# A diagonal matrix product in a chunked scan: the decayed state goes into PSUM, and the results are evacuated as copies

## The chip, the cores and the metric

The kernel runs on one core of one Trainium2 chip. The metric is device time of one execution in microseconds (us), as a median over runs. The engines are TensorE (PE in the profile, with its weight loads as PEld), VectorE (DVE), ScalarE (ACT), GpSimd (POOL) and SyncE (SP), which issues the DMAs.

## The reference, cut to what matters

The program is a two-layer encoder over 512 tokens and 1024 channels. The change sits in layer 0, in the RWKV-7 time mixing: 8 heads of 64 channels, two directions, with a recurrence over the tokens for a 64 x 64 state per head and direction.

```python
def step(S, inp):
    r_t, w_t, k_t, v_t, kk_t, a_t = inp
    sa = jnp.einsum('dbhvk,dbhk->dbhv', S, kk_t)
    S = (S * w_t[..., None, :] - sa[..., :, None] * (kk_t * a_t)[..., None, :]
         + v_t[..., :, None] * k_t[..., None, :])
    return S, jnp.einsum('dbhvk,dbhk->dbhv', S, r_t)
...
_, ys = lax.scan(step, S0, seqs)
ys = jnp.moveaxis(ys, 0, 2)
y = ys[0] + jnp.flip(ys[1], axis=1)
```

Beside it, in the same layer, stand an input projection, a Hyena branch (long convolutions through transforms) and an output projection; then come a gated MLP, an embedding, a second layer with attention, and a second MLP and embedding.

## The kernel before, in words

Channels lie on the 128 partitions, tokens along the free axis. `mixer0` is the whole mixing part of layer 0; everything after it is a chain of large products in float32r (three matmuls for one product of split numbers, tile names `g`, `whi`, `wlo`). In `mixer0` the code doesn't write its instructions in a fixed order. A class `Pace` keeps estimates of when each engine will be free and each tile be ready, and `drive` writes, step by step, either a piece of the **main line** (dense products: the input projection, the transforms, per-layer embeddings, the early part of the output projection `out_early`, the inverse transforms `inverse`) or a stage of one of the **chains** of small steps. `in_order` then holds every engine to the order in which it was written. So a change of one chain's instructions moves the places of all others in the four queues. SBUF work tiles there come from a pool of slabs (`SLABS`, name `w`), PSUM tiles from a pool of 8 banks (name `b`).

The recurrence is computed in chunks of 64 tokens. For two heads at a time (`m` = 0 to 3) and both directions, `rwkv_prep` makes the decayed vectors, `inverse_ab` inverts triangular matrices, and `scan(m)` goes through 8 chunks, each of which needs the state of the one before. `next_scan` lets at most two scans be open. When a scan is over, `rwkv_out(m)` makes its part of the output projection's input.

One chunk of `scan`, before, in the order in which it is written (`uv` holds state and values, `x` what was prepared, `ch` a PSUM tile with three slots for each direction, `yp` the outputs' PSUM tile; "product" is a group of four 64-row or 128-row matmuls, one for each direction and head):

1. first product (`m1` with `uv`) into slot 0; DVE copies it to `r0` (L1281);
2. output product of the old state into `yp`; DVE makes `sp`, the state times its decay (L356, two instructions, one per head; the decay is in `pcs`);
3. second product (`zt` with `r0`) into slot 1; ACT writes one head's negated result into `uv`, DVE the other's (L1296);
4. third product (`x` with `uv`) into slot 2; DVE adds `sp` to it and writes the new state into the next chunk's `uv` (L356, two instructions);
5. the rest of the outputs into `yp`.

A helper records most operations, so that in the profile all `self.mm` have line 350, all `self.tt` line 356 and all `self.act` line 359; tile names tell them apart. The tile `r0` is called `r` in the profile, as buffer numbers are left out.

Of the kernel before, what the change touches and what calls it, by code (L numbers as in the profile page):

```python
# [10 lines left out]
F32 = mybir.dt.float32  # L11
# [21 lines left out]
# ---------------------------------------------------------------- layout of the weights  # L33
# [14 lines left out]
# row tiles of layer 0's output projection: those of its early part, and the others  # L48
# [20 lines left out]
def _kc(n):  # L69
    """Row tiles of weights in a chunk of n column tiles."""  # L70
    return (8, 4, 2, 2)[n - 1]
# [13 lines left out]
# columns of the packed per-channel parameters: name -> number of columns  # L85
# [32 lines left out]
# ---------------------------------------------------------------- constants of the shapes  # L118
# [23 lines left out]
def _constants():  # L142
# [18 lines left out]
    # transforms at the frequencies (2f+1)pi/1024, f < 256; even and odd times apart, which gives those of 511 - f  # L161
# [4 lines left out]
    fwd = parts.reshape(4, 4, P, 2, P)  # part, tile of times, time, fc, f  # L166
    c["dft_f"] = np.ascontiguousarray(fwd.transpose(3, 2, 0, 1, 4)).reshape(2, P, 2048)
    inv = parts.transpose(0, 2, 1).reshape(4, 2, P, S)  # part, fc, f, time
    c["dft_i"] = np.ascontiguousarray(inv.transpose(1, 2, 0, 3)).reshape(2, P, 2048)
    # filter features and decay window  # L170
# [10 lines left out]
def _rpb_table(rpb):  # L181
    """Relative position bias as each (16-column query block, head) reads it, both by columns of the grid;
    -1e30 outside the window."""
# [16 lines left out]
    t = np.stack(out, axis=2).reshape(8, 2, P, 3, 256)  # pair, head, q, table, key  # L200
# [3 lines left out]
# ---------------------------------------------------------------- the kernel  # L204
class Pace:
    """Estimates of when what is written so far will have run. The order in which the rest is written follows them;
    nothing that is computed depends on them."""
# [15 lines left out]
    @staticmethod  # L223
    def area(x):
        """Name, first and last row, first and last column."""
        size = math.prod(x.tensor.shape[1:])
        p, f = divmod(x.offset, size)
        p1, f1 = p, f
        for i, (step, n) in enumerate(x.ap):
            if i == 0 and step == size:  # L230
                p1 += n - 1
            elif step < 0:
                f += step * (n - 1)
            else:
                f1 += step * (n - 1)
        return x.tensor.name, (p, p1, f, f1)
# [5 lines left out]
    def ready(self, tiles):  # L242
        """When all that is written into the tiles so far is there."""
# [4 lines left out]
    def after(self, marks, area, e, own):  # L248
        """The end of the accesses in marks to an area, seen by engine e; those of its own count only if own."""
# [10 lines left out]
    # TensorE runs at half its clock after a stretch of this many us in which it streamed less than so many columns  # L260
# [5 lines left out]
    def density(self, t):  # L266
        """Columns streamed in the last TICK us before t."""
# [48 lines left out]
class Kern:  # L316
# [5 lines left out]
    # -- helpers  # L322
# [26 lines left out]
    def mm(self, out, lhsT, rhs, start=True, stop=True):  # L349
        return self.nc.tensor.matmul(out, lhsT, rhs, start=start, stop=stop)  # L350
# [10 lines left out]
    def split(self, h, l, src, scale=None):  # L361
        """h + l = src (* scale), each in float32r."""
# [12 lines left out]
    def load_split(self, src, width, dt=F32):  # L375
        """One chunk of weights: from DRAM and into its two parts."""
# [7 lines left out]
    def gemm(self, wname, g, k0, k1, xs, evac, then=None):  # L384
        """then: what goes in between after two chunks of weights."""
# [23 lines left out]
    def rsqrt_rows(self, pool, srcs, col, scale, eps):  # L409
        """For each of srcs [128 channels, tokens]: 1 / sqrt(scale * (sums over the channels of col) + eps),  # L410
        back on all of those channels, in PSUM."""
# [23 lines left out]
    def norm(self, h, gain):  # L435
        """Splits gain * h into float32r parts; returns them, the tile of 1 / rms per token, on all partitions,
        and what computes that."""
# [25 lines left out]
    def conv3(self, out, u, w, b):  # L463
        """Centred depthwise convolution of width 3 over the tokens."""
# [9 lines left out]
    # -- the whole  # L474
# [42 lines left out]
    def mixer0(self):  # L517
# [5 lines left out]
        # tiles in DRAM  # L523
# [31 lines left out]
    SLABS = 59  # L555
    PREPS = 4

    def in_order(self, start):
        """Keeps the compute engines to the order in which everything from instruction start on is written."""
# [11 lines left out]
    # -- small helpers: slabs of SBUF, a bank of PSUM  # L571
# [9 lines left out]
    def parts(self, src):  # L581
        """A slab's two parts; the second one by GpSimd."""
# [5 lines left out]
    def stream(self, items):  # L588
        """Slabs from DRAM in their two parts, loaded and split ahead of their use. An item with two sources has its
        parts in them."""  # L590
# [37 lines left out]
    def weights(self, name, g):  # L628
        """The slabs of a group of columns."""
# [15 lines left out]
    # -- the order of the work: a main line of dense products, and chains of small steps beside it  # L645
    def start(self, prio, gen, *wait):
        """A chain of stages. It yields what its next stage waits for; of the chains whose stages can go, the one of
        the lowest prio does."""
# [3 lines left out]
    def put(self, out, in_):  # L652
        """A store, written once its data should be there, so that its queue doesn't wait."""
# [16 lines left out]
    def drive(self):  # L670
        """Stages of the chains as they can go, and the main line between them."""
# [31 lines left out]
    def both_mixers(self):  # L703
# [32 lines left out]
        # [chunk of frequencies][cosine, sine][f, 511 - f]  # L736
# [40 lines left out]
        # loads in the order of their use  # L777
# [24 lines left out]
        # 1 - mu; k_a / 2 and 1 - k_a / 2; w0 / 2, a0 / 2  # L802
# [24 lines left out]
    def norm0(self, xin):  # L827
        """The layer's input with its gains, in two parts; 1 / rms per token."""
# [30 lines left out]
    def columns(self, out):  # L859
        """A tile of columns of the input projection."""  # L860
# [986 lines left out]
```

## Time and profile before

| | |
|---|---|
| time, median of 3 runs | 1636.56 us (1633.0 to 1638.45) |
| the profiled execution | span 1633.0 us, which is also its time |
| PE busy | 1541.6 us (94%), 9296 matmuls |
| DVE busy | 1047.9 us (64%) |
| ACT busy | 681.0 us (42%) |
| POOL busy | 341.3 us (21%) |
| `mixer0` | from 0 to about 504 us; the four scans lie in 180 to 484 us |

Busy time of an engine is the sum of its instructions' times; matmuls overlap in their pipeline and their ends are modelled, so that a busy PE is not a PE at its peak. Idle time "before" a group of instructions is put down to the instruction that ended the wait. In a timeline, rows that follow each other closely are merged (`x8` is 8 instructions; a 64 x 64 float32 matmul is recorded as two).

### The profile page before, as it was taken

To read this page: it belongs to the slowest core of one execution; us is meant where nothing else is said; L and a number is where in the kernel's file an instruction comes from. 1 tells how busy PE (TensorE), PEld (TensorE's weight loads), DVE (VectorE), ACT (ScalarE), POOL (GpSimd) and SP (SyncE) were. 2 spreads that over 40 slices of the span, in tenths; PEclk is the share of its full clock that TensorE was granted. 3 is DMA by queue.
4 is the path that set the end of the run, shared out by engine and by line. 5 is a ranking of instruction groups with operands and counts; after the bars stand their busy time and mean duration, and the time that the engine had idled before them with its cause. 6 is when DMAs were issued, how large, how long until landed. Compare 5 with 4: busy or idle time off the path is not lost.

```text
span 1633.0 us, 24094 instructions
## 1 busy us (share of the span) xinstructions
PE 1541.6 (94%) x9296; PEld 1216.2 (74%) x9296; DVE 1047.9 (64%) x1740; ACT 681.0 (42%) x1082; POOL 341.3 (21%) x286
## 2 busy tenths in 40 slices
PE   7998798979898999999999989999999999999997
PEld 4675576766667888888888778777777888888886
DVE  7579868876876677534684664565666665276654
ACT  6464224333514544313443553565554442144432
POOL 3585525533721200000001322011030000000020
PEclk9999899899999999999999999999999999999999
DMA  6455638465764232222322433323112332322341
GB/s 202 136 141 137 188 105 237 136 215 157 232 214 167 100 103 90 96 99 90 103 91 96 137 116 103 106 83 123 66 65 78 103 104 90 98 88 93 110 142 65
DMA packets 116308, 200.13 MB, mean 123 GB/s; under 512 B 27729, under 2 KB 57297, under 8 KB 116194
## 3 DMA queue, kind: packets, MB, share of 16 engines
q1 hardware_dynamic: 116194, 198.59, 37.9%
q8 instruction: 73, 1.20, 0.3%
q14 instruction: 41, 0.34, 0.1%
HBM read 166.04 MB, written 30.93 MB: 121 GB/s over the span
## 4 chain that ended last, share of the span: by engine, by line
PE 76%; DVE 11%; issue 5%; ACT 3%; DMA 2%; POOL 2%; SPq 2%; POOLq 0%; DVEq 0%; ACTq 0%
PE g L350 60%; PE b L350 11%; DVE w L356 4%; DVE w L353 3%; PE m L350 1%; PE s L350 1%; PE m L1792 1%; ACT w L359 1%; POOL w L356 1%; DVE w L1168 1%; POOL rr L356 0%; ACT oh L364 0%; DVE ol L356 0%; DMA ch_d<-w 0%; POOL nacc L356 0%
## 5 line engine op out<-in xcount | busy, mean ns | idle before, releaser
L356 DVE TENSOR_TENSOR wlo<-wraw,whi 128x1024 fp32r<-128x1024 f32 x186 | 235.6, 1268 | 334.7 <-ACT whi L364 334.5
L364 ACT CAST whi<-wraw 128x1024 fp32r<-128x1024 f32 x186 | 194.2, 1044 | 426.8 <-PE g L350 410.2
L350 PE MATMUL g<-xh,whi 128*128 128x512 f32 x872 | 341.5, 392 | 5.4 <-ACT whi L364 5.4
L350 PE MATMUL g<-xl,whi 128*128 128x512 f32 x872 | 340.5, 390 | 0.0
L350 PE MATMUL g<-xh,wlo 128*128 128x512 f32 x872 | 340.3, 390 | 0.0
L356 POOL TENSOR_TENSOR w<-w 128x512 fp32r<-128x512 f32 (+2 forms) x142 | 184.0, 1317 | 166.7 <-ACT w L584 95.8
L350 PEld LDWEIGHTS g<-xh,whi 128*128 128x128 f32 x872 | 164.2, 188 | 41.2 <-ACT whi L364 5.6
L350 PEld LDWEIGHTS g<-xh,wlo 128*128 128x128 f32 x872 | 164.1, 188 | 34.9 <-DVE wlo L356 0.8
L350 PEld LDWEIGHTS g<-xl,whi 128*128 128x128 f32 x872 | 164.3, 188 | 33.7
L350 PE MATMUL b<-xh,w 128*128 128x512 f32 x464 | 172.4, 427 | 7.4 <-ACT xh L359 7.3
L356 POOL TENSOR_TENSOR nacc<-nsq 128x512 f32<-128x512 f32 x5 | 9.3, 1865 | 779.8 <-ACT nsq L359 779.8
L350 PE MATMUL b<-w 64*64 64x64 f32 (+6 forms) x1884 | 131.2, 271 | 17.5 <-DVE w L353 7.5
L350 PE MATMUL g<-hh,wlo 128*128 128x512 f32 x352 | 139.0, 395 | 0.0
L350 PE MATMUL g<-hl,whi 128*128 128x512 f32 x352 | 139.0, 395 | 0.0
L350 PE MATMUL g<-hh,whi 128*128 128x512 f32 x352 | 138.9, 395 | 0.0
L353 DVE SCALAR_TENSOR_TENSOR c<-u,prm,c 128x511 f32<-128x511 f32 x176 | 126.6, 748 | 6.9 <-ACT c L359 6.3
L350 PEld LDWEIGHTS b<-w 64*64 64x64 f32 (+4 forms) x1884 | 94.6, 142 | 44.1 <-POOL w L356 10.4
L350 PEld LDWEIGHTS b<-xh,w 128*128 128x128 f32 x464 | 91.6, 197 | 36.8 <-ACT xh L359 8.0
L359 ACT ACTIVATE c<-u,prm 128x512 f32<-128x512 f32 x88 | 70.0, 817 | 71.4 <-DVE u L356 71.4
L350 PE MATMUL b<-xl,w 128*128 128x512 f32 x232 | 95.7, 413 | 1.6 <-DVE xl L353 1.4
L356 DVE TENSOR_TENSOR w<-w 128x512 f32<-128x512 f32 (+16 forms) x127 | 88.8, 708 | 3.8 <-DMA w<-hw_d 1.0
L356 DVE TENSOR_TENSOR u<-g,rstd 128x512 f32<-128x512 f32 x104 | 71.5, 687 | 14.2 <-PE g L350 13.4
(178 smaller groups left out, 2344.0 us busy)
## 6 DMA issues: line engine op xcount, KB each, us to landing
wraw<-in_up SPq DMA_DIRECT2D x88, 512.0 KB, 3.5
wraw<-in_down SPq DMA_DIRECT2D x44, 512.0 KB, 3.4
w<-in_mix_w_in SPq DMA_DIRECT2D x52, 256.0 KB, 3.8
wraw<-in_na_w_qkv SPq DMA_DIRECT2D x24, 512.0 KB, 3.5
x<-ch_d SPq DMA_DIRECT2D x16, 640.0 KB, 5.9
ch_d<-w SPq DMA_DIRECT2D x64, 128.0 KB, 2.7
wraw<-in_gate SPq DMA_DIRECT2D x16, 512.0 KB, 3.5
tab<-in_rpb SPq DMA_DIRECT2D x8, 768.0 KB, 4.3
```

The costliest lines, as they stand in the source:

```text
L350: return self.nc.tensor.matmul(out, lhsT, rhs, start=start, stop=stop)
L353: return self.nc.vector.scalar_tensor_tensor(out=out, in0=in0, scalar=scalar, in1=in1, op0=op0, op1=op1)
L356: return (eng or self.nc.vector).tensor_tensor(out=out, in0=in0, in1=in1, op=op)
L359: return self.nc.scalar.activation(out=out, in_=in_, func=func, **kw)
L364: self.nc.scalar.copy(h, src)
L1168: nc.vector.tensor_reduce(out=x[:, i, 0:i], in_=tv, axis=AX.X, op=ALU.add)
L1792: nc.tensor.transpose(pst[:, i], sc[:, i // 2, (i % 2) * P:(i % 2 + 1) * P], ident)
```

## The change

Three things change, all in `scan` but for the size of the pool. The decayed state is no longer made by DVE: `decay(c)` lets ACT write, one chunk ahead, a matrix `dg` with the chunk's decay on its diagonal (the identity, scaled by a column of `pcs`), and a new product of `dg` with the state goes into slot 2 of `ch`, where the third product is then accumulated onto it. The copy to `r0` goes from DVE to ACT. The new state is evacuated by one copy on ACT (first head) and one on DVE (second head), in place of two additions on DVE. Only the first matmul into a bank half has its start flag now, since all slots share a bank. The pool of slabs has one fewer, since the four `dg` tiles (1 KB a partition each) are larger than the four `sp` tiles (512 bytes).

```diff
-    SLABS = 59
+    SLABS = 58
...
+        def decay(c):
+            if c < 7:
+                dg = dgs[c] = rb.tile([P, 2, P], F32, name="dg", bufs=4)
+                for d in range(2):
+                    self.act(dg[:, d], self.cst("ident"), AF.Copy, scale=self.pcs[:, m, d, c:c + 1])
+        decay(0)
...
-                    self.mm(ch[rows, d, 0], m1[d][par][:, c], uv[:, d, par, w])
+                    self.mm(ch[rows, d, 0], m1[d][par][:, c], uv[:, d, par, w], start=d == 0, group=False)
+            if c < 7:
+                dg = dgs.pop(c)
+                for d in range(2):
+                    for par, rows in both:
+                        self.mm(ch[rows, d, 2], dg[rows, d, rows], uv[rows, d, par, w], False, group=False)
...
-            nc.vector.tensor_copy(out=r0, in_=ch[:, :, 0])
+            nc.scalar.copy(r0, ch[:, :, 0])
...
-            if c < 7:
-                sp = rb.tile([P, 2, 64], F32, name="sp", bufs=4)
-                for par, rows in both:
-                    self.tt(sp[rows], uv[rows, :, par, w],
-                            self.pcs[rows, m, :, c].unsqueeze(2).to_broadcast([64, 2, 64]), ALU.mult)
...
-                    self.mm(ch[rows, d, 1], zt[d][rows, c], r0[rows, d])
+                    self.mm(ch[rows, d, 1], zt[d][rows, c], r0[rows, d], False, group=False)
...
+            decay(c + 1)
             yield uv,
...
-                        self.mm(ch[rows, d, 2], x[:, d, par, o], uv[:, d, par, w])
-                for par, rows in both:
-                    self.tt(nx[rows, :, par, wn], ch[rows, :, 2], sp[rows], ALU.add)
+                        self.mm(ch[rows, d, 2], x[:, d, par, o], uv[:, d, par, w], False, group=False)
+                nc.scalar.copy(nx[0:64, :, 0, wn], ch[0:64, :, 2])
+                nc.vector.tensor_copy(out=nx[64:128, :, 1, wn], in_=ch[64:128, :, 2])
```

In the changed file these lines stand some 10 lines lower: the copy to `r0` is L1298, DVE's negation L1308, the new state's copies L1317 (ACT) and L1318 (DVE).

How the queues move is shown at the sixth chunk of the last scan (m = 3). The PSUM tile `ch` of that chunk is `b_5419` before and `b_5529` now; brackets name the engine whose signal an instruction waits for.

PE before, from the chunk's first product (`uv,w`) to the next chunk's. `x,uv` is an output product, `r,w` the second product, `uv,x` the third; `xh` and `xl` are a piece of `out_early` from the main line.

```order
L350 MATMUL b<-uv,w 64x64 x4
L350 MATMUL b<-x,uv 64x64 x4
L350 MATMUL b<-r_5424,w 64x64 x4
L350 MATMUL b<-xh_3898,w 128x512
L350 MATMUL b<-xl_3899,w 128x512
L350 MATMUL b<-xh_3898,w 128x512
L350 MATMUL b<-xh_4419,w 128x512
L350 MATMUL b<-xl_4420,w 128x512
L350 MATMUL b<-xh_4419,w 128x512
L350 MATMUL b<-uv,x 64x64 x4
L350 MATMUL b<-x,uv 64x64 x4
L350 MATMUL b<-uv,w 64x64 x4
```

PE now, from the sixth chunk's first product to the seventh's `dg` product:

```order
L350 MATMUL b<-uv,w 64x64 x4
L350 MATMUL b<-uv,dg 64x64 x4
L350 MATMUL b<-x,uv 64x64 x4
L350 MATMUL b<-r_5538,w 64x64 x4
L350 MATMUL b<-uv,x 64x64 x4
L350 MATMUL b<-x,uv 64x64 x4
L350 MATMUL b<-uv,w 64x64 x4
L350 MATMUL b<-uv,dg 64x64 x4
```

The new product (`uv,dg`) stands between the first product and the outputs', and at this chunk the six dense matmuls that lay between the second and the third product lie elsewhere.

ACT before, from the fifth chunk's negated result to the seventh's: casts of transform and embedding tiles, copies of outputs, and one instruction of the scan for each chunk.

```order
L584 CAST w_5382<-w_5359 128x512 [waits DVE_49]
L584 CAST w_5386<-w_5360 128x512 [waits DVE_49]
L359 ACTIVATE uv_5011<-b_5368 64x2x64 [waits DVE_49,PE_49]
L359 ACTIVATE uv_5011<-b_5419 64x2x64 [waits DVE_49,PE_49]
L359 ACTIVATE uv_5011<-b_5456 64x2x64 [waits DVE_49,PE_49]
```

ACT now, the sixth chunk alone:

```order
L1298 COPY r0_5538<-b_5529 128x128 [waits PE_49]
L359 ACTIVATE uv_5095<-b_5529 64x2x64 [waits PE_49,Activation_49]
L359 ACTIVATE dg_5551<-con_58,pcs_144 128x128 x2
L584 CAST w_5554<-w_5455 128x512 [waits DVE_49]
L584 CAST w_5558<-w_5456 128x512 [waits DVE_49]
L1317 COPY uv_5095<-b_5529 64x2x64 [waits DVE_49,PE_49]
```

ACT has five instructions of the scan for a chunk in place of one, and here two casts stand ahead of its copy of the new state.

DVE before, the sixth chunk:

```order
L1281 COPY r0_5424<-b_5419 128x128 [waits PE_49]
L356 TENSOR_TENSOR sp_5430<-uv_5011,pcs_144 64x128 [waits DVE_49] x2
L1296 TENSOR_SCALAR uv_5011<-b_5419 64x2x64 [waits DVE_49,Activation_49]
L356 TENSOR_TENSOR uv_5011<-b_5419,sp_5430 64x2x64 [waits PE_49]
L356 TENSOR_TENSOR uv_5011<-b_5419,sp_5430 64x2x64
```

DVE now, the sixth chunk and the seventh's negation:

```order
L1308 TENSOR_SCALAR uv_5095<-b_5529 64x2x64 [waits DVE_49,Activation_49]
L356 TENSOR_TENSOR w_5562<-w_4914,w_4915 128x512 [waits DMAHW0_49]
L356 TENSOR_TENSOR w_5563<-w_4914,w_4915 128x512 [waits DMAHW2_49]
L1318 COPY uv_5095<-b_5529 64x2x64 [waits Activation_49]
L1308 TENSOR_SCALAR uv_5095<-b_5584 64x2x64 [waits DVE_49,Activation_49]
```

Of DVE's six instructions for a chunk two are left, and both wait for ACT: the negation as before, and the copy of the new state, whose signal comes from ACT's copy of the other head. An addition and a subtraction of the spectrum now stand between the two.

More of the change, by code (lines that the diff above doesn't have):

```diff
@@ L347, in rcst, with mm @@
         return self.rcon[:, a:b]
-    def mm(self, out, lhsT, rhs, start=True, stop=True):
-        return self.nc.tensor.matmul(out, lhsT, rhs, start=start, stop=stop)
+    def mm(self, out, lhsT, rhs, start=True, stop=True, group=True):
+        return self.nc.tensor.matmul(out, lhsT, rhs, start=start, stop=stop, skip_group_check=not group)
     def stt(self, out, in0, scalar, in1, op0, op1):
@@ L1270, in scan @@
         yts = None
+        dgs = {}
+        def decay(c):
[4 more added lines that the diff above has]
+        decay(0)
         for c in range(8):
```

## The prediction

> **What bounds the kernel now.** I read the page first: with its instructions' times added up PE is busy for 94% of the span, but the change touches only the scans, so I cut the span where scans start and end.
>
> ```profile
> span 1633.0 us, 24094 instructions
> PE 1541.6 (94%) x9296; PEld 1216.2 (74%) x9296; DVE 1047.9 (64%) x1740; ACT 681.0 (42%) x1082; POOL 341.3 (21%) x286
> ```
>
> The busy times by stretch (length, then PE, PEld, DVE, ACT, POOL, then granted clock, DMA share and GB/s):
>
> ```profile
> 0.00:180.00 180.00, 155.41 (x1101) 111.59 (x1101) 138.14 (x222) 93.00 (x161) 109.17 (x117) 0.95 0.53 155
> 180.00:252.00 72.00, 63.70 (x859) 46.68 (x858) 51.48 (x125) 19.15 (x43) 23.87 (x21) 0.95 0.54 157
> 252.00:365.00 113.00, 95.56 (x1045) 72.55 (x1043) 94.24 (x184) 39.87 (x80) 54.08 (x49) 0.91 0.62 186
> 365.00:437.00 72.00, 67.36 (x652) 51.73 (x653) 54.13 (x108) 30.40 (x63) 34.44 (x27) 0.93 0.56 174
> 437.00:504.00 67.00, 54.53 (x509) 41.24 (x507) 50.24 (x91) 21.14 (x43) 25.58 (x19) 0.96 0.62 213
> 504.00:1633.00 1129.00, 1105.09 (x5136) 892.45 (x5136) 659.69 (x1015) 477.44 (x694) 94.15 (x56) 0.99 0.30 100
> ```
>
> The last 1129 us hold no scan and keep their instructions. The four stretches with scans last 324 us: PE busy 281.2 (87%), DVE 250.1 (77%), ACT 110.6 (34%), and PE idle 42.9. PE is the fullest, DVE close behind, ACT has room. The waits of PE there (in total, times, longest) name who makes it idle:
>
> ```profile
> PE b L350 <- DVE uv L356: 11.1, 15, 3.0
> PE b L350 <- DVE w L356: 7.0, 6, 2.6
> PE b L350 <- DVE uv L1296: 6.0, 5, 2.7
> PE b L350 <- DVE r L1281: 5.5, 5, 1.9
> PE g L350 <- ACT whi L364: 5.4, 1, 5.4
> PE b L1043 <- DVE w L356: 2.8, 1, 2.8
> ```
>
> So 22.6 us (11.1 + 6.0 + 5.5) are waits for the scan's own three DVE steps, and 9.8 us (7.0 + 2.8) for other DVE work; the 5.4 us stand at the end, where the large products begin. A chain that is merely busy on DVE costs nothing where the main line fills PE; these waits are what can be won.
>
> One chunk that runs undisturbed, the sixth of the last scan, from its first product to the next one's (start, duration, engine, line, tiles, in brackets the idle time before):
>
> ```profile
> 472.75 0.77 PE L350 MATMUL b<-uv,w 128*64 128x64 f32 x8 [0.23 <-DVE uv L356]
> 473.45 0.45 PE L350 MATMUL b<-x,uv 64*64 64x64 f32 x8
> 473.55 0.29 DVE L1281 COPY r<-b 128x128 f32<-128x128 f32 x1 [0.54 <-PE b L350]
> 473.88 0.60 DVE L356 TENSOR_TENSOR sp<-uv,pcs 64x128 f32<-64x128 f32 x2
> 473.90 0.45 PE L350 MATMUL b<-r,w 64*64 64x64 f32 x8
> 474.28 0.50 PE L350 MATMUL b<-xh,w 128*128 128x512 f32 x1
> 474.39 0.27 ACT L359 ACTIVATE uv<-b 64x128 f32<-64x128 f32 x1 [3.85 <-PE b L350]
> 474.70 0.29 DVE L1296 TENSOR_SCALAR uv<-b 64x128 f32<-64x128 f32 x1 [0.22 <-ACT uv L359]
> 475.87 0.45 PE L350 MATMUL b<-uv,x 128*64 128x64 f32 x8
> 476.37 0.61 DVE L356 TENSOR_TENSOR uv<-b,sp 64x128 f32<-64x128 f32 x2 [1.38 <-PE b L350]
> 476.71 0.66 PE L350 MATMUL b<-uv,w 128*64 128x64 f32 x6 [0.15 <-DVE uv L356]
> ```
>
> Here `sp` is off the path: it ends at 474.48, before ACT's negation ends at 474.66. And a chunk with DVE's queue full, the first of the same scan:
>
> ```profile
> 440.21 2.32 DVE L356 TENSOR_TENSOR sp<-uv,pcs 64x128 f32<-64x128 f32 x2
> 442.64 0.29 DVE L1296 TENSOR_SCALAR uv<-b 64x128 f32<-64x128 f32 x1
> 442.97 6.36 DVE L356 TENSOR_TENSOR w<-w 128x512 f32<-128x512 f32 x4
> 442.99 0.45 PE L350 MATMUL b<-uv,x 128*64 128x64 f32 x8 [1.29 <-DVE uv L1296]
> 449.36 0.61 DVE L356 TENSOR_TENSOR uv<-b,sp 64x128 f32<-64x128 f32 x2
> 449.70 0.77 PE L350 MATMUL b<-uv,w 128*64 128x64 f32 x8 [3.04 <-DVE uv L356]
> ```
>
> The first wait (1.29) came from a slow `sp` ahead of the negation, and goes with `sp`; the second (3.04) from four other DVE operations ahead of the new state, and nothing in the change takes those away.
>
> **The change part by part.** The groups that it removes or that price what it adds (busy, mean ns, idle before):
>
> ```profile
> L356 DVE TENSOR_TENSOR sp<-uv,pcs 64x128 f32<-64x128 f32 x56 | 21.5, 384 | 1.3
> L356 DVE TENSOR_TENSOR uv<-b,sp 64x128 f32<-64x128 f32 x56 | 16.0, 286 | 9.3 <-PE b L350 8.2
> L1296 DVE TENSOR_SCALAR uv<-b 64x128 f32<-64x128 f32 x32 | 9.4, 294 | 12.9 <-ACT uv L359 12.2
> L1281 DVE COPY r<-b 128x128 f32<-128x128 f32 x32 | 9.2, 287 | 12.4 <-PE b L350 12.4
> L359 ACT ACTIVATE uv<-b 64x128 f32<-64x128 f32 x32 | 8.7, 270 | 120.5 <-PE b L350 104.0 <-DVE sp L356 16.5
> L1314 ACT COPY w<-b 128x256 f32<-128x256 f32 x16 | 5.2, 376 | 10.5 <-PE b L350 10.5
> L584 ACT CAST w<-w 128x512 fp32r<-128x512 f32 x53 | 31.7, 618 | 8.8 <-DVE w L356 5.0 <-DMA w<-in_mix_w_out_a 1.9 <-DMA s_d<-w 1.8
> ```
>
> 1. *The new product.* 28 groups of four (7 chunks in each of 4 scans). Four such products take PE from 473.90 to 474.28, 0.38 us: 28 x 0.38 = +10.6. They stand behind the first product, and the copy to `r0` now waits for all eight, as they share a PSUM tile; so they lie on the scan's path as well as on PE. Low end 6, if PE would else have stood waiting at some of them; high end 13, at the lower granted clock (0.91) and with some cold stretches. I take 10.6. The Trainium skill ("PSUM — Partial Sum Buffer", on bank collisions) says that two engines must not be on the same bank and quadrant at once, whatever the address, so the copy could not go ahead of the new product even with other bookkeeping; no run here shows the collision.
>
> 2. *DVE's relief.* Gone are 21.5 + 16.0 + 9.2 = 46.7 us; added are 28 copies at 0.29 (the nearest rows, 64x128 and 128x128 from PSUM, are 0.286 to 0.294) = 8.1. DVE falls from 250.1 to 211.5 us, 77% to 65% of the stretches. What PE gets of it lies between two ends: its 32.4 us of waits on DVE shrink in proportion to DVE's load (15%), -5; or the waits for `r0` (5.5) and the negation (6.0) vanish and half of those for the new state (5.5) do too, -17. The two waits of the disturbed chunk are one of each kind, so I take about the middle, -12.
>
> 3. *ACT's load.* Added are 32 copies to `r0`, 28 of the new state and 56 halves of `dg`. 128 elements in a row cost 0.27 on ACT and 256 cost 0.376; at 0.28 that makes 116 x 0.28 = +32.5 us, ACT from 34% to 44%. `dg` is written one chunk ahead and needed later than the two instructions take (0.56): its cover is the third product, which in the undisturbed chunk starts 1.2 us after ACT's negation ends. If that cover goes, the new state's copy comes late by up to 0.5 us. What is new is that the scan's copies queue behind casts of 0.62, some of which wait for a DMA. An even chance of meeting half a cast (0.44 x 0.31 us), twice a chunk, would be 7.6 us over 28 chunks; most of it falls where PE has dense work. Between 0 and 6 I take +2.
>
> 4. *The new state through two engines.* Two additions in a row took 0.61 us. Now ACT copies one half (0.27) and then DVE, which waits for ACT, the other (0.29); with the 0.04 us that the negation shows between the two (474.66 to 474.70) that is 0.60. Nothing won, nothing lost: 0.
>
> 5. *The granted clock.* The stretches ran at 0.91 to 0.96: 72 x 0.05 + 113 x 0.09 + 72 x 0.07 + 67 x 0.04 = 21.5 us of full clock lost. With a third less waiting some of it comes back: -2.5 (0 to -5).
>
> 6. *One slab fewer, and the order.* No row prices the slab. SP's queue already waits where a weight load needs a slab that PE still reads:
>
> ```profile
> SPq L599 <- PE b L350: 12.5, 10, 3.7
> ```
>
> Yet the casts of such a weight (the L584 row) waited for it only 1.9 us. 0, up to +3. The last scan's last chunk now has 35 dense units of the main line (matmuls of 512 columns) behind it on PE, before 53: 18 units at 0.23 us (474.62 to 474.85 in the same chunk) have moved ahead of it. The cover of the final `rwkv_out` gets shorter by 4.1 us; it stays covered if the inverse transform still ends later. 0, up to +4.
>
> Sum: +10.6 - 12 + 2 + 0 - 2.5 + 0 = -1.9 us on the profiled execution of 1633.0, so 1631.1. The median of the runs (1636.56) lies 3.6 above that execution; set beside it: 1634.7, and I say 1634.5.
>
> **The rivals.**
>
> *DVE was the real bound.* In the second stretch DVE is busy for 83% and PE for 85%, and every wait of PE in the list above but the last stage's 5.4 us is on DVE. The slow `sp` (its 56 took 271 to 1265 ns) speaks for a queue whose waits fall faster than its load:
>
> ```profile
> L356 DVE TENSOR_TENSOR sp<-uv,pcs x56: 271/289/1265, 188.9 to 478.2; 64x128 f32<-64x128 f32 x56
> ```
>
> Then the high ends of steps 2 and 5 hold and the 9.8 us of other waits halve: 10.6 - 17 - 4.9 - 5 + 1 = -15, 1621. Against it: the undisturbed chunk, where DVE isn't on the path but for `r0`. The Trainium skill ("SBUF — State Buffer", Who interferes with whom) has it that a DVE instruction with two SBUF inputs contends with GpSimd's reads; the trace agrees, as `sp` reads two SBUF tiles and swings by a factor of 4.7, while the copy to `r0` and the negation, which read PSUM, don't.
>
> *The two halves of the new state go side by side.* They touch different partitions. Then 0.3 us a chunk are won, 28 x 0.3 = -8.4, and the time is 1626. Against it: DVE's negation, the same pattern, waited 12.2 us for ACT's (row of L1296), and the copy's signal comes from ACT. The Trainium skill's PSUM page would let two engines work in different quadrants of a bank at once; that permits this rival, but the built order doesn't use it.
>
> *Slower: the chain gets longer than the plan thinks.* The planner compares areas, sees two halves on different partitions and reckons ACT's and DVE's copies side by side, so it expects the new state 0.3 us too early in each of 28 chunks; at chunks where it leaves no dense work between (as in the sixth of the last scan) PE stands. Price: 8.4, with +10.6 of the new product and only the proportional -5 of waits: +14, 1650. It decides from where PE's waits at the scan shrink by less than about 6 us in total. For it: ACT's negation and DVE's already run in series; against it: dense work fills most of these gaps.
>
> **How the numbers follow.** What a measurement can tell from no change here is about 0.3%, 4.9 us: 1631.7 to 1641.5 is "the same". The forecast, a balance of more PE work and fewer waits, 0.38. DVE the bound, 0.31, and side by side, 0.05, both faster: 0.36. The longer chain, 0.26, slower. Low end 1622, next to the DVE rival's 1621; high end 1648, next to the chain's 1650. The forecast's own range is 1630 to 1641.
>
> **What would show it.** In the new profile: `dg` matmuls as 224 records, each four spaced by 0.38 us (step 1); DVE in `mixer0` lower by about 38 us, PE's waits for DVE's `uv` and ACT's `r` together near 12 us in place of 22.6 (2); ACT higher by 32 us, its copies at 0.27 to 0.29 (3); DVE's copy starting after ACT's (4); a granted clock in 180 to 500 us above 0.94 (5); the first `g` matmul at 501 to 504 us. I'm wrong if other waits, on ACT's queue or on weights, take the place of those removed, or if the new order of the main line leaves a hole of several us anywhere.

## The result and the profile after

The changed kernel takes 1652.71 us (1650.82 to 1654.92), the kernel before 1635.64 us (1633.0 to 1638.45): ratio 1.0099, 95% interval 1.0080 to 1.0117. It is slower by 1%; 1634.5 was forecast. The order in which the planner wrote the new instructions makes the loss; the instructions by themselves cost next to nothing, as two runs with swapped orders show below.

The page after, to be read against the same two lines of before:

```profile
span 1651.0 us, 24581 instructions
PE 1553.8 (94%) x9520; PEld 1223.8 (74%) x9520; DVE 1008.0 (61%) x1624; ACT 711.4 (43%) x1198; POOL 337.0 (20%) x286
```

DVE fell by 39.9 us and ACT rose by 30.4, as forecast (38 and 32); PE's busy time rose by 12.2. So the edit did its work on the engines, and the span is 18 us longer all the same. Where? The stretches of the changed kernel (length, then PE, PEld, DVE, ACT, POOL, granted clock, DMA share, GB/s), the last two being all of the scans' part up to the first `g` matmul, and the rest:

```profile
180.00:252.00 72.00, 61.64 (x855) 45.16 (x846) 44.32 (x95) 25.10 (x69) 22.99 (x21) 0.95 0.52 149
252.00:365.00 113.00, 96.00 (x997) 71.02 (x997) 71.86 (x127) 44.26 (x102) 48.51 (x46) 0.86 0.53 156
365.00:437.00 72.00, 61.74 (x600) 45.63 (x600) 41.23 (x87) 31.57 (x78) 24.31 (x20) 0.88 0.64 191
180.00:522.61 342.61, 293.72 (x3236) 219.83 (x3227) 209.68 (x389) 140.29 (x341) 130.17 (x113) 0.91 0.56 173
522.61:1651.00 1128.39, 1104.56 (x5136) 891.43 (x5136) 659.42 (x1016) 477.28 (x694) 94.14 (x56) 0.99 0.30 100
```

and the same two of before:

```profile
180.00:503.99 323.99, 281.14 (x3060) 212.19 (x3059) 250.08 (x505) 110.56 (x229) 137.97 (x113) 0.93 0.59 182
503.99:1633.00 1129.01, 1105.10 (x5136) 892.46 (x5136) 659.70 (x1015) 477.44 (x694) 94.15 (x56) 0.99 0.30 100
```

The rest is the same (1128.4 against 1129.0), so all 18.6 us lie in the scans' part. PE is busy there for 12.6 us more and idle for 6.0 more (48.9 against 42.9). The new product accounts for about half of the busy time (PE is busy for 6.7 us more in e1 below, which has the product but not the new order); the granted clock fell from 0.91 to 0.86 between 252 and 365 us and from 0.93 to 0.88 between 365 and 437. PE's waits in the scans' part of the changed kernel:

```profile
PE b L350 <- DVE uv L1318: 7.5, 7, 4.1
PE b L350 <- DVE w L356: 7.1, 4, 4.3
...
PE b L350 <- DVE w L1168: 5.2, 2, 4.9
...
PE b L350 <- ACT uv L1317: 4.9, 6, 1.3
PE b L350 <- ACT dg L359: 3.3, 2, 2.0
PE b L350 <- DVE uv L1308: 2.4, 7, 0.8
```

The scan's own steps are waited for less than before: 7.5 + 4.9 + 2.4 = 14.8 us (18.1 with the 3.3 for `dg`), where `r`, negation and new state had 22.6. But waits of 4 to 5 us stand here that before did not have (its longest on DVE was 3.0): for the new state's DVE half (4.1), for other DVE work (4.3, 4.9). The 4.9 stands at the start of the first scan (182 us); the two others come in the middle, 13 us apart.

The longest wait for the new state, in the timeline of the changed kernel (start, duration, engine, line, tiles, in brackets the idle time before):

```profile
313.63 0.29 DVE L1308 TENSOR_SCALAR uv<-b 64x128 f32<-64x128 f32 x1 [2.10 <-ACT uv L359]
...
313.96 5.12 DVE L353 SCALAR_TENSOR_TENSOR w<-w,prm 128x511 f32<-128x511 f32 x4
...
314.55 0.26 ACT L1317 COPY uv<-b 64x128 f32<-64x128 f32 x1 [0.95 <-PE b L350]
...
319.06 0.33 PE L350 MATMUL b<-uv,w 128*64 128x64 f32 x2
...
321.73 1.42 DVE L356 TENSOR_TENSOR w<-b,rcon 128x256 f32<-128x256 f32 x4
...
323.17 0.29 DVE L1318 COPY uv<-b 64x128 f32<-64x128 f32 x1
...
323.52 0.69 PE L350 MATMUL b<-uv,w 128*64 128x64 f32 x6 [4.13 <-DVE uv L1318]
```

ACT's half of the new state is there at 314.81. DVE's half is one copy of 0.29 us, and it runs 8.4 us later, because 9.2 us of other work (313.96 to 323.17) stand ahead of it in DVE's queue: four operations of the Hyena branch, six of the inverse of another pair, and four multiplications by a mask (the row at 321.73). The main line's dense matmuls cover 4.4 us of that (to 319.06), and PE stands for 4.13. It stands again some 13 us later:

```profile
334.68 0.69 DVE L356 TENSOR_TENSOR w<-w,rcon 128x512 f32<-128x512 f32 x1 [3.91 <-DMA vt_d<-w]
...
337.10 2.08 PE L350 MATMUL b<-w,con 128*128 128x512 f32 x2 [4.33 <-DVE w L356]
```

for 4.33, on a chain whose DVE operation the profile puts behind a store. Now the clock around both:

```profile
314.00:319.00 5.00, 5.00 (x35) 3.84 (x34) 4.93 (x4) 0.78 (x2) 3.43 (x3) 1.00 0.19 64
324.00:328.70 4.70, 4.70 (x34) 2.88 (x32) 1.85 (x5) 1.79 (x4) 0.00 (x0) 0.50 0.75 223
328.80:332.70 3.90, 3.90 (x25) 3.22 (x25) 0.80 (x2) 3.87 (x8) 1.69 (x2) 1.00 0.27 25
337.10:342.40 5.30, 5.30 (x43) 3.52 (x45) 2.00 (x3) 1.13 (x2) 2.19 (x3) 0.50 0.67 163
342.50:346.00 3.50, 3.50 (x68) 2.71 (x64) 3.46 (x6) 1.24 (x3) 0.05 (x1) 1.00 0.78 243
310.00:346.00 36.00, 26.14 (x239) 18.89 (x239) 22.11 (x38) 11.25 (x24) 13.75 (x13) 0.81 0.47 125
```

PE is full again from 324 us on, but at half clock for 4.7 us, and again for 5.3 us behind the second wait: a wait is paid for twice, once standing and once running slowly behind it. In these 36 us (the last row) PE stands for 9.9 us, and at least 10.0 us of its work run at half clock, which costs 5.0 more. The Trainium skill ("TensorE: Matmul & The Clock Gate", HAM oscillation — how this bites in real kernels) says that the clock is halved when TensorE stands idle for more than about 3.4 us; the rows agree for these two waits, 4.13 and 4.33 us with 0.50 behind each. But the same trace has 0.50 behind a wait of only 1.24 us too (last section), so a wait here needn't be that long.

### The profile page after: what moved, and what is told of

Read it like the earlier page. It is cut to its first block, busy times and chain, and to the rows that moved or that the text cites. A ratio compares the mean times of both kernels' runs of the same rounds, so it can differ in the third digit from the quotient of the medians.

```text
span 1651.0 us, 24581 instructions
## 1 busy us (share of the span) xinstructions
PE 1553.8 (94%) x9520; PEld 1223.8 (74%) x9520; DVE 1008.0 (61%) x1624; ACT 711.4 (43%) x1198; POOL 337.0 (20%) x286
## 4 chain that ended last, share of the span: by engine, by line
PE 66%; DVE 2%; ACT 2%; DMA 1%; issue 1%; POOL 1%; POOLq 0%; SPq 0%; DVEq 0%; ACTq 0%
PE g L350 60%; PE b L350 2%; PE s L350 1%; PE m L350 1%; PE m L1805 1%; DVE w L356 1%; ACT oh L364 0%; DVE ol L356 0%; DMA w<-in_mix_w_out_a 0%; DMA w<-in_xT 0%; POOL rr L356 0%; POOL nacc L356 0%; PE m L1756 0%; DVE u L356 0%; ACT xh L359 0%
## 5 line engine op out<-in xcount | busy, mean ns | idle before, releaser
L356 POOL TENSOR_TENSOR w<-w 128x512 fp32r<-128x512 f32 (+2 forms) x142 | 179.7, 1284 | 189.3 <-ACT w L584 145.6
L350 PE MATMUL b<-w 64*64 64x64 f32 (+6 forms) x1884 | 135.1, 275 | 20.7 <-DVE w L353 13.2
L356 DVE TENSOR_TENSOR w<-w 128x512 f32<-128x512 f32 (+16 forms) x127 | 83.1, 662 | 4.1 <-ACT w L1327 1.3
L356 DVE TENSOR_TENSOR u<-g,rstd 128x512 f32<-128x512 f32 x104 | 71.2, 685 | 14.3 <-PE g L350 13.4
```

Of the source, the lines that this page charges most:

```text
L356: return (eng or self.nc.vector).tensor_tensor(out=out, in0=in0, in1=in1, op=op)
```

## The experiments

Ratios are to the kernel before, timed beside each.

| run | instructions | order | time, us | ratio, 95% interval |
|---|---|---|---|---|
| changed kernel | changed | its planner's | 1652.71 | 1.0099, 1.0080 to 1.0117 |
| e1 | changed | of before | 1638.19 | 1.0011, 0.9998 to 1.0025 |
| e2 | before | of after | 1659.36 | 1.0132, 1.0107 to 1.0157 |
| e3 | before | planned again, HOP 0.22 | 1654.53 | 1.0107, 1.0089 to 1.0125 |
| e4 | changed | planned, costs told | 1654.49 | 1.0108, 1.0089 to 1.0126 |
| e5 | product alone | of before | 1641.02 | 1.0027, 1.0012 to 1.0043 |
| e6 | before, `r0` on ACT | of before | 1631.95 | 0.9977, 0.9961 to 0.9992 |
| e7 | changed | planned, HOP 0.22 | 1658.80 | 1.0132, 1.0113 to 1.0152 |
| e8 | changed | planned, SLACK 0.3 | 1646.17 | 1.0057, 1.0038 to 1.0077 |
| e9 | before, `r0` and negation on ACT | of before | 1624.05 | 0.9919, 0.9905 to 0.9933 |
| e10 | changed | of before to scan 1, then planned | 1648.94 | 1.0076, 1.0062 to 1.0090 |
| e11 | changed | of before through scan 1, then planned | 1648.24 | 1.0065, 1.0044 to 1.0087 |
| e12 | before, `r0` on ACT | planned again | 1653.58 | 1.0106, 1.0092 to 1.0120 |

### Orders swapped: e1 and e2

All that the planner decides from its estimates (which chain goes next, whether the main line goes first, when a store or a weight load is issued) was written down as a list for each kernel, and the other kernel reads its decisions from the list:

```diff
-            x = next((x for x in self.chains
-                      if (x[0] < 1.8 or not lag) and pace.ready(x[2]) <= now + self.SLACK), None)
-            if pace.cold(now) or pace.density(now) < self.WARM:
+            k = self.ask(lambda: next((k for k, x in enumerate(self.chains)
+                      if (x[0] < 1.8 or not lag) and pace.ready(x[2]) <= now + self.SLACK), -1))
+            x = self.chains[k] if k >= 0 else None
+            if self.ask(lambda: int(pace.cold(now) or pace.density(now) < self.WARM)):
```

(and so at the other places where it decides). `ask` takes the next entry of the list and leaves the planner's own answer unused:

```diff
+    def ask(self, value):
+        return ASKED.popleft()
```

Expected of e1:

> The changed kernel's instructions, written in the order of stages that the planner chose for the kernel before: every choice that it makes from its estimates (which stage or piece of the main line next, which load to split, which store to write) is replaced by the choice recorded there, so that GpSimd's and the DMA queue's rows are those of before and the other queues differ only inside the scan's stages. If the loss comes from the new order (theory A), the time comes back to within 5 us of the 1635.6 of before. If it comes from the instructions themselves (theory B: 28 more products, a longer chain, ACT's share), it stays near 1652, 10 to 20 us above before.

and of e2:

> The other way round: the instructions of the kernel before (state decayed and added on DVE, copy to r0 on DVE, 59 slabs), written in the order of stages that the planner chose for the changed kernel. Theory A: the loss comes along with the order, 1645 to 1660. Theory B: about 1636, as nothing of the change's work is in it.

Measured: the changed instructions in the old order 1638.19, the old instructions in the new order 1659.36. So with the instructions fixed the new order costs 14.5 us (1652.7 against 1638.2) or 22.8 (1659.4 against 1636.6, the kernel before beside it); with the old order fixed the change costs 1.6 us, an interval of -0.3 to +4.1 us by the ratio. That the order makes the loss is shown. In the new order the changed instructions are 6.7 us faster than the old ones (5.4 by the ratios, whose intervals overlap). In e1, in the 36 us where the changed kernel stood and in the scans' part (lines are some 17 to 25 higher than in the changed kernel: the new state's copies are L1342 and L1343):

```profile
310.00:346.00 36.00, 34.14 (x487) 26.12 (x485) 25.56 (x37) 13.51 (x33) 13.52 (x15) 1.00 0.40 119
180.00:510.70 330.70, 287.85 (x3235) 217.64 (x3227) 213.92 (x390) 139.67 (x341) 133.37 (x113) 0.93 0.58 179
```

The clock is 1.00 where the changed kernel had 0.81. Against e1 the changed kernel's scans' part is 11.9 us longer: PE idle 48.9 against 42.9 (6.0) and busy 293.7 against 287.9 (5.9) for the same matmuls. Half of what the order costs is standing, half is the clock: PE's busy time times the share of the clock that was missing, worked out for each half microsecond of the scans' part and added up, gives 25.0 us in the changed kernel and 19.2 in e1, and what is left of the busy time is the same in both (268.8 and 268.7).

The place can be named too. From 310 to 346 us e1 stands for 1.9 us and loses nothing to the clock, where the changed kernel stands for 9.9 and loses at least 5.0, so 13.0 us between them. That is all of the 11.9; elsewhere the two about balance, and e1 has waits of 4.6 us (at 182) and 4.1 us (at 290) of its own. So a long wait by itself doesn't tell the two orders apart; what does is the sum of idle time and slow work. The same chunk in e1 (the seventh of scan 1):

```profile
321.50 0.30 DVE L1333 TENSOR_SCALAR uv<-b 64x128 f32<-64x128 f32 x1 [2.10 <-ACT uv L376]
...
325.71 0.29 DVE L1343 COPY uv<-b 64x128 f32<-64x128 f32 x1
...
326.22 0.45 PE L367 MATMUL b<-uv,w 128*64 128x64 f32 x8
```

Here DVE's copy stands 4.2 us behind its negation in place of 9.5, and the matmul behind it waits for nothing: the main line had enough dense work in between.

### A nudge of the planner: e3, e7 and e8

```diff
-    HOP, OWN = 0.2, 0.13
+    HOP, OWN = 0.22, 0.13
```

in the kernel before (e3) and the changed one (e7), and in the changed one

```diff
-    SLACK = 0.2
+    SLACK = 0.3
```

(e8). HOP is the planner's estimate of a signal from engine to engine.

> A control: the kernel before, with one constant of the planner's estimates moved (a hop between engines 0.22 in place of 0.20 us). The same instructions in another order. If orders that the planner finds equally good differ on the chip by several us (theory A needs that), this one lies more than 4 us away from 1635.6, either way. If the order hardly matters, it lies within 4 us.

> The changed kernel with the planner's estimate of a hop between engines at 0.22 us in place of 0.20: the instructions stay, the order is planned again. If the changed kernel's loss is one unlucky order among many (theory: order), this falls anywhere between about 1640 and 1665, as the same nudge moved the kernel before by +18. If the loss is in the instructions, it stays within 5 us of 1652.7.

> The changed kernel with the planner's slack at 0.3 us in place of 0.2 (a step of a chain may be written when its inputs are due up to 0.3 us late): instructions as in the changed kernel, another order. By the theory of the order: anywhere from 1640 to 1665, with the place of scan 2's and scan 3's first copies moving by several us. By the theory of the instructions: 1648 to 1657.

With 0.02 us more in one estimate the kernel before takes 17.9 us more (1654.53 against 1636.58), as much as the whole change; the changed kernel moves by +6 and by -7 us with the two nudges, both outside the ranges that were named for a loss made by the instructions (within 5 us of 1652.7, and 1648 to 1657). The time of any version whose order is planned afresh is uncertain by more than the terms that my sum was made of.

### The planner told the true costs: e4

```diff
-            if p <= q1 and q <= p1 and f <= g1 and g <= f1:
+            if (p <= q1 and q <= p1 or name.startswith("uv") and k != e) and f <= g1 and g <= f1:
...
-            return 0.08 + n * 0.0009
+            return 0.08 + n * 0.0009 + (0.194 if self.name(ins.outs[0].bass_ap).startswith("dg") else 0.0)
```

The planner now reckons that accesses of two engines to the halves of `uv` go one after the other, and that a half of `dg` takes 0.39 us; its other estimates stay as they were. This is the test of my rival "the chain gets longer than the plan thinks".

> The changed kernel, with the planner told what the trace of the changed kernel shows: one half of dg takes 0.39 us on ACT, where it reckoned 0.195, and the copies and negations of the two heads on ACT and DVE follow each other, where it reckoned them side by side. Theory C (the loss is an order that follows wrong estimates of the scan): 1636 to 1645. Theory B: 1650 to 1655, as the work stays. Theory A in its general form, orders by luck: anywhere between 1635 and 1660.

1654.49, no better than 1652.71. That rival named a time close to the one that came (1650), but its mechanism isn't the cause: with these two estimates set right the loss stays, and in the old order, with the same chain, there is none. The time falls into the range named for theory B, the instructions, but e1 excludes that theory; it fits the general form of A. That some other wrong estimate steers the planner badly isn't excluded.

### Parts of the change in the old order: e5, e6 and e9

With the order held the parts can be weighed. e5, the changed kernel with all three copies on DVE:

```diff
-            nc.scalar.copy(r0, ch[:, :, 0])
+            nc.vector.tensor_copy(out=r0, in_=ch[:, :, 0])
...
-                nc.scalar.copy(nx[0:64, :, 0, wn], ch[0:64, :, 2])
+                nc.vector.tensor_copy(out=nx[0:64, :, 0, wn], in_=ch[0:64, :, 2])
```

> The order in which the kernel before is written is held, and of the change only the new product is made: dg is built on ACT and multiplied on PE, while the copy to r0 and both copies of the new state are DVE's. Against the earlier run of the whole change in that order (1638.2, kernel before 1636.6) this tells what moving the copies to ACT was worth. Step 1 and step 2 of the prediction: +10.6 for the product, and DVE relieved only by the 56 products sp (21.5 us of 46.7, so about half of the -12): 1636.6 + 10.6 - 6 = about 1641. If the product lies on the scan's path and no relief counts: about 1647. If it fills time in which PE waits anyway: about 1636.

e6, the kernel before with one line of the change:

```diff
-            nc.vector.tensor_copy(out=r0, in_=ch[:, :, 0])
+            nc.scalar.copy(r0, ch[:, :, 0])
```

> The kernel before with one edit, the copy to r0 on ACT in place of DVE, in the order of the kernel before. There is no new product, so this prices the relief of DVE by itself. By step 2 the waits of PE on r (5.5 us) go and the others shrink a little: about -5, 1631 to 1633. If ACT's queue makes the copy as late as DVE's did, 1636 to 1638. If every wait is already covered by the order: 1636.

The product alone costs 0.27% (4.4 us at the ratio; 1641.02, expected about 1641 by the prediction's steps 1 and 2), and `r0` on ACT alone wins 0.23% (3.8 us; 1631.95, expected 1631 to 1633). That e5 met its number is in part luck: it was summed up from a product priced too dear and a relief priced too high (step by step below). The change is a good half and a bad half, and together they come out near nothing: e1. The split of the new state's copies over two engines was not run by itself. e6 with the second half of the negation on ACT too is e9:

```diff
-            nc.vector.tensor_scalar(out=uv[64:128, :, 1, w], in0=ch[64:128, :, 1], scalar1=-1.0,
-                                    scalar2=None, op0=ALU.mult)
+            self.act(uv[64:128, :, 1, w], ch[64:128, :, 1], AF.Copy, scale=-1.0)
```

> The kernel before in its own order, with two edits: the copy to r0 on ACT (worth -0.23% by itself in the run before this one), and the second half of the negation on ACT too, right behind the first; no new product. With r0 alone PE still waited 6.1 us for DVE's half of the negation, which ran behind ACT's half anyway. If DVE's queue is what made that half late: another -3 to -6, about 1627. If two instructions of 0.27 us in a row on ACT cost what the hop to DVE cost: 1632 as with r0 alone. If ACT's queue becomes the bound: 1635 or more.

1624.05 us, 0.81% faster than the kernel before (ratio 0.9919, 0.9905 to 0.9933), the fastest version here. The scans' part and PE's waits on the scan's steps, first e6, where L1321 is DVE's half of the negation:

```profile
180.00:499.76 319.76, 280.50 (x3057) 210.34 (x3049) 237.31 (x473) 118.62 (x261) 134.50 (x113) 0.94 0.60 186
```

```profile
PE b L367 <- DVE uv L373: 11.4, 17, 3.3
PE b L367 <- DVE uv L1321: 6.1, 5, 3.7
```

then e9:

```profile
180.00:493.35 313.35, 277.43 (x3068) 208.98 (x3066) 234.31 (x444) 131.01 (x296) 133.35 (x113) 0.95 0.62 190
```

```profile
PE b L367 <- DVE uv L373: 10.0, 15, 2.6
PE b L367 <- ACT uv L376: 5.2, 4, 3.6
```

Each row moves a little in the right direction; of the 6.4 us that the scans' part gets shorter, 3.1 are less busy time of PE (280.5 to 277.4) for the same matmuls and 3.3 less idle time (39.3 to 35.9). The busy time is the clock again: worked out as for e1, the missing clock costs 16.8 us in e6 and 13.4 in e9. The mechanism that I expected (the negation no longer waited for) is only 0.9 us of the gain, since ACT's negation is now waited for instead. The gain is measured, and by the medians (7.9 us) larger than the 3 to 6 us that were expected; what makes the rest I haven't separated.

### Where in the order: e10 and e11

The changed kernel reads the list of before up to a point, and from there decides for itself:

```diff
+        return ASKED.popleft() if ASKED else value()
```

> The changed kernel; up to the start of scan 1 its instructions stand in the order of the kernel before, and from there the planner decides by itself, with the changed kernel's numbers. In the changed kernel scan 1 ended within 4 us of the kernel before and the loss of 14 us showed between the end of scan 1 and the start of scan 2. If that loss is made by the order written from scan 1 on, it comes again: 1648 to 1660. If it came from the order up to scan 1 (a debt that shows later): about 1638.

> As the kernel above, but the order of the kernel before is kept to the end of scan 1; the planner decides only what is written behind it (scans 2 and 3). If the loss is made by what is written during scan 1: most of it is gone, 1638 to 1643. If the planner's order of scans 2 and 3 costs as much by itself: 1646 to 1655.

e10, 1648.94, agrees with a loss that is made from scan 1 on. In e11 scan 1 has its good order and the hole at 319 us is avoided, but 1648.24 is still 0.65% over the kernel before: the second of the two cases, in which the order of scans 2 and 3 costs as much by itself. Its six runs lie between 1640.7 and 1651.2, two of them at 1641, so the size of this loss is not certain. So the hole that I showed is one form of the loss and not its only place: plan scans 2 and 3 afresh, and most of a loss of that size is made there.

### A gain that a new plan hides: e12

The edit of e6, with the order left to the planner.

> The kernel before with the copy to r0 on ACT alone, as in the run at 0.9977, but with its order planned again by the kernel's own planner and not held. If the order outweighs an edit of this size: anywhere from 1638 to 1660, so the same edit that is faster in the old order comes out slower. If the loss of the changed kernel belongs to its instructions: 1630 to 1636, as in the old order.

The same line that wins 0.23% in the old order loses 1.06% in the order that the planner makes for it. Its scans' part and PE's longest sum:

```profile
180.00:524.40 344.40, 283.52 (x3004) 212.56 (x2996) 237.68 (x468) 117.85 (x259) 130.84 (x112) 0.90 0.56 171
365.00:437.00 72.00, 52.63 (x560) 40.52 (x559) 42.70 (x93) 21.64 (x50) 20.32 (x16) 0.79 0.52 162
```

```profile
PE b L350 <- DVE uv L356: 26.4, 18, 4.5
```

There the waits for the new state alone are 26.4 us, and a stretch of 72 us runs at 0.79. No diagonal product and no split copy is in this kernel, and its time is that of the changed one.

## Why the prediction was wrong, step by step

The step that failed is the sixth, "one slab fewer, and the order", put at 0 and at most +7 (3 for the slab, 4 for the cover of the last output). The order is worth +14.5 us with the changed instructions. I priced one cover, of 4.1 us, at the end of the last scan; the loss lies in the middle, from 310 to 346 us, in two waits of 4.13 and 4.33 us and in the half clock behind each. I had named it as what would prove me wrong (a new order that leaves a hole of several us), without giving it a chance of its own. The first `g` matmul, forecast at 501 to 504 us, came at 522.61.

With the order held, the sum of the steps, -1.9, stands against a measured +1.8 (the ratio of e1; -0.3 to +4.1). That it comes so near is in part luck: the product was priced too dear, and what it was to be paid with too high. If the product is worth the 7.8 us of step 1 below, +1.8 leaves about -6 for steps 2 to 5 together (an estimate), where I had -12.5. The steps:

1. The new product, +10.6, was too dear. Four products lie 0.28 us apart (319.83 to 320.11 in e1), not 0.38, so 28 x 0.28 = 7.8; PE's busy time in the scans' part rose by 6.7 in e1. The rows, which also show that the copy to `r0` waits for all eight products (the four first ones and the four of `dg`):

```profile
319.83 0.45 PE L367 MATMUL b<-uv,dg 64*64 64x64 f32 x8
320.11 0.40 PE L367 MATMUL b<-x,uv 64*64 64x64 f32 x8
320.32 0.27 ACT L1323 COPY r<-b 128x128 f32<-128x128 f32 x1 [3.97 <-PE b L367]
```

   The copy starts at 320.32, when the eight (with the pipeline's modelled end at 320.28) are done, though what it reads was ready before them.

2. DVE's relief, -12, was mis-sized. DVE fell as forecast. In e1 PE waits for DVE's copy and negation in `uv` 8.4 and 3.6 us and for `r` not at all: 12.0, where "near 12" in place of 22.6 was forecast. So these waits went as I said, but that was not the time won: other waits stand in their place, 1.6 us for ACT's copy of the new state, 3.5 for `dg`, 4.6 for a load at the start of the first scan, and PE's idle time in the scans' part is 42.9 us in the traces of both e1 and the kernel before.

```profile
PE b L367 <- DVE uv L1343: 8.4, 7, 2.8
...
PE b L367 <- DMA uv<-vt_d: 4.6, 1, 4.6
...
PE b L367 <- DVE uv L1333: 3.6, 6, 2.7
PE b L367 <- ACT dg L376: 3.5, 3, 2.0
```

   The two traces can't price the relief: e1's profiled execution (1642.4) is 4.2 us over its median, that of before (1633.0) 3.6 under its own.

3. ACT's load, +2, was mis-sized in the part for `dg`: `dg` isn't a copy of 0.28 us. The rows of the changed kernel (the first has least, median and largest duration in ns, the others busy time, mean and idle time before):

```profile
L359 ACT ACTIVATE dg<-con,pcs x56: 387/389/438, 178.8 to 495.3; 128x128 f32<-128x128 f32 x56
```

```profile
L1298 ACT COPY r<-b 128x128 f32<-128x128 f32 x32 | 8.5, 265 | 81.5 <-PE b L350 81.5
L1317 ACT COPY uv<-b 64x128 f32<-64x128 f32 x28 | 7.2, 257 | 21.8 <-PE b L350 14.1 <-DVE w L356 7.7
```

   A half takes 0.389 us, and PE waits for it 3.5 us in e1 (3.3 in the changed kernel), where I let the third product cover it. The copies to `r0` (0.265) and of the new state (0.257) came as priced. The Trainium skill ("ScalarE: Activation LUTs", What ACT_TABLE_LOAD costs) has the price that I missed: each operand that is a column of 128 values adds about 93 ns, and with one of them it gives 280 ns + 0.833 ns an element, for 128 an estimate of 387 ns; the row agrees, with 387 at least and 389 in the median. The rows from which I priced it have a constant scale or none.

4. The new state through two engines, 0: right. DVE's copy comes after ACT's, and where DVE's queue is empty the pair takes 0.26 + 0.03 + 0.29 = 0.58 us in place of 0.61:

```profile
496.57 0.26 ACT L1317 COPY uv<-b 64x128 f32<-64x128 f32 x1
...
496.86 0.29 DVE L1318 COPY uv<-b 64x128 f32<-64x128 f32 x1 [0.15 <-ACT uv L1317]
```

   The rival of two halves side by side did not happen.

5. The granted clock, -2.5, did not come. It was 0.93 in e1's scans' part, as before, and 0.91 in the changed kernel, so there it went the other way: the missing clock costs 18.6 us before, 19.2 in e1 and 25.0 in the changed kernel (worked out as for e1 above). Fewer waits for the scan's steps did not raise it, and PE's idle time did not fall.

6. The order: above. The slab itself is no part of it, since e1 and e5 have one fewer too and stay within 0.3% of the kernel before.

The rival "DVE was the real bound" is refuted for this change: DVE's load fell by 16% in the scans' part (250.1 to 209.7 us; to 213.9 in e1), and nothing was won even in the old order. It is half right as a reading: a wait for DVE here can mean that a short copy stands behind long work in DVE's queue, and moving single copies off that queue (e6, e9) does win. The list on which I read that nearly every wait of before is on DVE ended early: two waits of 2.7 us in total for a DMA and one of 1.3 for GpSimd come behind it.

What stays open is why the kernel before has an order that none of the eight new plans tried here (two nudged on the changed kernel, one on the kernel before, one with costs told, one with an edit of one line, two partly planned, and the changed kernel's own) reaches. That its numbers were chosen for its own instructions would explain it; no run shows it. The loss is also not put down to one decision of the planner: e11 shows that it comes again elsewhere.

## What to carry to other kernels

When a program writes its own order from estimates, an edit measured with the plan made afresh measures the plan: hold the order (record its decisions and read them back), weigh the edit, and only then plan again. Add up all of PE's idle time and the clock behind it, stretch by stretch, and not only the waits of the chain that was changed: here those fell while the whole got longer. And ask of each short copy on a step-by-step chain what stands ahead of it in its engine's queue. Of a change with several parts measure the parts: here the line that wins was bound to a product that costs as much.

## What the runs showed of the hardware that I had not expected

A wait costs more than its length. Behind the wait of 4.13 us PE worked at a granted clock of 0.50 for 4.7 us from 324 us on, and behind the one of 4.33 us for 5.3; in e1, without these waits, the clock was 1.00 there. About half of what the order cost (5.9 of 11.9 us) is this.

Short waits can do the same. In the changed kernel PE was busy for 2.04 of the 3.41 us up to 277.55, its longest wait there 1.24 us, and the next 6.82 us ran at 0.50; in the kernel before it was busy for 1.55 of the 3.41 us up to 279.96, with one wait of 1.86 us, and the next 3.41 us ran at 0.50. The rows, first of the changed kernel:

```profile
274.14:277.55 3.41, 2.04 (x34) 1.31 (x32) 0.99 (x2) 2.36 (x6) 1.86 (x2) 1.00 0.89 140
277.55:284.37 6.82, 6.82 (x44) 5.56 (x40) 5.85 (x14) 5.54 (x13) 4.78 (x5) 0.50 0.76 295
```

then of the kernel before:

```profile
276.55:279.96 3.41, 1.55 (x21) 0.98 (x19) 3.18 (x9) 0.00 (x0) 1.99 (x2) 1.00 0.74 179
279.96:283.37 3.41, 3.41 (x56) 3.17 (x56) 2.08 (x6) 0.78 (x2) 0.41 (x1) 0.50 0.41 167
```

In the scans' parts of these two traces and of e1's the clock is 1.00 or 0.50, and each time at 0.50 lasts 3.4 us or two, three or four times as long. The stretch of 3.41 us ahead of each had PE busy for 2.3 us or less; how little work it takes, no run here measures.
